# Loading and splitting the second-stage forget-gate weights at another place in a one-core hybrid decoder layer

## The chip, the cores and the metric

The kernel runs on one core of one Trainium2 chip. The metric is device time in microseconds (us) of one execution; several executions give a median. Five engines run side by side, each with its own instruction stream in a fixed order: TensorE (PE, with its weight loads shown apart as PEld), VectorE (DVE), ScalarE (ACT), GpSimd (POOL) and SyncE (SP), which here issues most of the DMAs. POOL issues DMAs too, on a queue of its own.

## What is computed

One decoder layer on 256 tokens of width 2048. A combined projection `h @ w_in` feeds two token mixers, a gated linear attention (GLA) and a differential attention; their outputs are gated, merged and projected again. The change touches the forget gate of the GLA, which is computed in two stages: a projection to rank 16, then a small matrix `w2` (16 x 1024).

```python
h = rmsnorm(x, pre_norm_g[l])
proj = h @ w_in[l]
(a_q, a_k, a_v, a_g, a_lr, b_q, b_k, b_v, b_g, m_a, m_b) = jnp.split(proj, offsets, axis=-1)
gk = jax.nn.log_sigmoid((a_lr @ gla_gk_w2[l] + gla_gk_b[l]).astype(jnp.float32)) / GATE_LOGIT_NORMALIZER
o_a = gla_chunked(
...
merged = jax.nn.sigmoid(m_a) * y_a + jax.nn.sigmoid(m_b) * y_b
out = merged @ w_out[l]
x = x + rmsnorm(out, post_norm_g[l])
```

## The kernel before

Every weight comes from DRAM as float32 and is split on the core into two parts for TensorE: `hi`, a rounded copy that ACT makes (line 263), and `lo = raw - hi`, which DVE makes (line 264). Inputs are split in the same way (`xs`), and a product is three matmuls: hi by hi, hi by lo, lo by hi. The unit of this work is a half tile: one `hi` and one `lo` of 128 x 832 elements in the first phases. `emit_half` makes one; `take` keeps three ahead of the matmuls (`AHEAD = 3`); there are three buffers for each of `raw`, `hi` and `lo`. A `raw` buffer holds two half tiles and is loaded again, on SP's queue, when DVE has made both `lo` parts.

The phases that matter here are the first ones:

- `first_joint` (line 428): 16 half tiles of `v0`, which holds the rank-16 columns and the first values. PE runs 12 matmuls for each (line 440).
- `token_major` (line 466, matmuls on line 452) for `v2` and then `v3`, 8 half tiles each. Between two half tiles `pump` advances side tasks that stand in the list `tasks`.
- From there the phase of the sets: `block_products`, whose weights go through four `chain` buffers (`a` and `b`, loaded by `link`, line 177), interleaved with `others`.

The side tasks are `load_constants` (line 323: identity, biases, masks, and at its end `w2`), `late` (norms and lambda), `forget_gate` (line 521) and `sum_operands` (line 597), which makes sums of blocks of the inputs (`temp`, in `chain` buffers) and splits them into `s4`, `r1`, `s2` and `r3` (lines 617 and 618).

`forget_gate` turns the rank-16 result (`lr`, line 526), splits it into `lrt` (lines 529 to 533), splits `w2_raw` into `w2_s` and `w2h` (lines 537 to 539: two ACT instructions and one DVE instruction that needs the second of them), multiplies (line 548, 8 matmuls of 256 columns), and evaluates the log-sigmoid on ACT and DVE (lines 551 to 564). `w2_raw` is 128 x 1024: the 16 rows of `w2` stand in it four times, at partitions 0, 32, 64 and 96, for the four combinations of hi and lo, and the other rows are zero.

A scheduling layer places each instruction in its engine's order when the program is built, by its dependencies and by what each engine has before it; `tc.keep_in_program_order` pins an instruction to the place that the code gives it. Tiles of one `tag` share a buffer: `w2_raw` has that of `s2h`, `w2h` that of `r3h`. DMAs that SP issues pass through eight completion counters in turn (DMAHW0 to 7), and an issue first waits until the DMA eight places before it has landed. In the profile's rows digits are left out of names: `w_raw` is `w2_raw`, `w_s` is `w2_s`, `w2h` stays.

Of the kernel before, what the change touches and what calls it, by code (L numbers as in the profile page):

```python
# [6 lines left out]
F32 = mybir.dt.float32  # L7
# [3 lines left out]
AF = mybir.ActivationFunctionType  # L11
ALU = mybir.AluOpType
AX = mybir.AxisListType

P = 128
# [7 lines left out]
RANK = 16  # L23
# [71 lines left out]
def hybrid_kernel(ctx: ExitStack, tc, xt, xn, preg, postg, w, w2, gkb, glag, lamv, diffg, ident_d, causal_d, lmask_d, out):  # L95
    nc = tc.nc
    pe, act, dve, pool, sp = nc.tensor, nc.scalar, nc.vector, nc.gpsimd, nc.sync
# [8 lines left out]
    blocks = joint.enter_context(tc.tile_pool(name="blocks", bufs=2))  # L106
# [3 lines left out]
    def u(shape, name, dtype=F32):  # L110
        count[0] += 1
        return big.tile(shape, dtype, tag="u", name=f"{name}_{count[0]}")

    def u2(shape, name, dtype=F32):
        count[0] += 1
        return pools[1].tile(shape, dtype, tag="u2", name=f"{name}_{count[0]}")

    def sm(shape, name, dtype=F32, bufs=2):
        count[0] += 1
        return pools[0].tile(shape, dtype, tag=name, name=f"{name}_{count[0]}", bufs=bufs)  # L120

    def t2(shape, name):
        count[0] += 1
        return pools[0].tile(shape, F32, tag="t2", name=f"{name}_{count[0]}", bufs=5 if len(pools) == 1 else 12)
# [12 lines left out]
    def ps(tag):  # L137
        count[0] += 1
        return psum.tile([P, 512], F32, tag=tag, name=f"{tag}_{count[0]}")

    def f32(ap):
        return ap.bitcast(F32)
# [175 lines left out]
    diffg_s = const.tile([P, 1], F32, name="diffg_s")  # L318
    lam_s = sm([P, 4, 64], "lam_s", bufs=1)

    w2_tile = []

    def load_constants():
        tc.keep_in_program_order(sp.dma_start(ident, ident_d))
        for t, src in ((gkb_s, gkb), (glag_s, glag), (diffg_s, diffg), (causal, causal_d)):
            tc.keep_in_program_order(sp.dma_start(t, src))
        tc.keep_in_program_order(sp.dma_start(lam_s, lamv.partition_broadcast(P)))
        yield
        for n in range(0, len(LEVELS) + 2, 4):
            m = min(4, len(LEVELS) + 2 - n)  # L330
            t = u([P, 4, S], "lmask")
            tc.keep_in_program_order(sp.dma_start(t[:, :m, :], lmask_d[:, n : n + m, :]))
            pool.tensor_copy(lmask[:, n : n + m, :], t[:, :m, :])
            yield
        w2_tile.append(lend("s2h", "w2_raw"))
        tc.keep_in_program_order(dve.memset(w2_tile[0], 0.0))
        for i in range(4):
            pool.dma_start(w2_tile[0][32 * i : 32 * i + RANK, :], w2)

    ones = const.tile([P, P], F32, name="ones")  # L340
    dve.memset(ones, 1.0)
# [36 lines left out]
    def norm_row():  # L378
        bank = ps("bg")
        for b in range(2):  # L380
            diag = sm([P, P], "diag")
            dve.tensor_scalar(out=diag, in0=ident, scalar1=rstd[:, b : b + 1], scalar2=None, op0=ALU.mult)
            pe.matmul(bank[:, P * b : P * b + P], ones, diag, start=True, stop=True)
        dve.tensor_copy(rstd_bc, bank[:, :S])

    def lam():
        late = tc.keep_in_program_order
        prod = sm([P, 2, 64], "lamp", bufs=1)
        for i in range(2):
            late(dve.tensor_tensor(out=prod[:, i, :], in0=lam_s[:, 2 * i, :], in1=lam_s[:, 2 * i + 1, :], op=ALU.mult))  # L390
        dots = sm([P, 2], "lamd", bufs=1)
        dve.tensor_reduce(out=dots, in_=prod, op=ALU.add, axis=AX.X)
        late(act.activation(dots, dots, AF.Exp))
        dve.tensor_scalar(out=neg_lam, in0=dots[:, 1:2], scalar1=dots[:, 0:1], scalar2=-LAM_INIT, op0=ALU.subtract, op1=ALU.add)
        dve.tensor_scalar(out=diffg_s, in0=diffg_s, scalar1=1.0 - LAM_INIT, scalar2=None, op0=ALU.mult)
# [120 lines left out]
    def lend(tag, name, dtype=F32):  # L516

        count[0] += 1
        return blocks.tile([P, 8, P], dtype, tag=tag, name=f"{name}_{count[0]}", bufs=1).rearrange("p a t -> p (a t)")

    def forget_gate():
        w2_raw = w2_tile[0]
        yield
        bank = ps("bg")
        for b in range(2):
            pe.transpose(bank[:, P * b : P * b + P], lr[:, b, :], ident)
        top = t2([P, 512], "lrh").bitcast(F32R)
        lrt = sm([P, S], "lrt", F32R, bufs=1)
        act.activation(top[:, :S], bank[:, :S], AF.Copy)
        for i in (0, 64):  # L530
            act.activation(lrt[i : i + 32, :], bank[i : i + 32, :S], AF.Copy)
            r = slice(i + 32, i + 64)
            dve.tensor_tensor(out=lrt[r, :], in0=bank[r, :S], in1=f32(top[r, :S]), op=ALU.subtract)
        w2_s = lend("s2l", "w2_s", F32R)
        top = lend("r3h", "w2h", F32R)
        r = slice(64, P)
        act.activation(w2_s[:64, :], w2_raw[:64, :], AF.Copy)
        act.activation(top[r, :], w2_raw[r, :], AF.Copy)
        dve.tensor_tensor(out=w2_s[r, :], in0=w2_raw[r, :], in1=f32(top[r, :]), op=ALU.subtract)
        yield  # L540
        gp.extend(u([P, 2, 4, P], "gp") for _ in range(2))
        for hf in range(2):
            for c in range(2):
                bank = ps("bg")
                for i in range(2):
                    ct = 4 * hf + 2 * c + i
                    o = bank[:, S * i : S * i + S]
                    pe.matmul(o, w2_s[:, P * ct : P * ct + P], lrt, start=True, stop=True)
                for i in range(2):
                    ct = 4 * hf + 2 * c + i  # L550
                    act.activation(gp[hf][:, :, 2 * c + i, :], bank[:, S * i : S * i + S].rearrange("p (b t) -> p b t", b=2), AF.Identity, bias=gkb_s[:, ct : ct + 1])
            yield
        e = [lend(tag, "e") for tag in ("r3h", "r3l")]
        z = [t.rearrange("p b c t -> p (b c t)") for t in gp]
        for hf in range(2):
            act.activation(e[hf], z[hf], AF.Abs)
            yield
            act.activation(e[hf], e[hf], AF.Exp, scale=-1.0)
            yield
        for hf in range(2):  # L560
            act.activation(e[hf], e[hf], AF.Ln, bias=1.0)
        for hf in range(2):
            yield
            dve.scalar_tensor_tensor(out=z[hf], in0=z[hf], scalar=0.0, in1=e[hf], op0=ALU.min, op1=ALU.subtract)
        done.add("gate")
# [71 lines left out]
    def late():  # L637
        norm_row()
        yield
        lam()  # L640
        yield

    tasks.append(load_constants())
    first_groups(first_joint())
    tasks.append(late())
    tasks.append(forget_gate())
    tasks.append(sum_operands())
    start = 2 * VG[0] - RANK
# [285 lines left out]
    for g in range(4):  # L934
        banks = token_major(f"ag{g}", 512, x_ops, 2)
        t = u2([P, 2, 512], "ua")
# [187 lines left out]
    for g in range(4):  # L1124
        banks = token_major(f"y1{g}", 512, b_ops, 1 if g else 2, None if g else settle)
        for b in range(2):
            t = gb[g][:, b, :]
# [11 lines left out]
    for b in range(2):  # L1139
        xres.append([])  # L1140
        for i in range(2):
            t = u([P, 1024], "xres")
# [126 lines left out]
```

## Time and profile before

| | |
|---|---|
| median of 3 runs | 1119.35 us (1118.45 to 1119.95) |
| span of the profiled execution | 1121.6 us |
| PE busy | 1101.9 us, 98% of the span |
| DVE busy | 851.3 us, 76% |
| ACT busy | 673.9 us, 60% |
| POOL busy | 111.2 us, 10% |
| DMA | 266.16 MB, mean 237 GB/s |
| PE's waits for other engines, all listed | 4.2 + 2.9 + 1.6 + 1.4 + 1.0 + 0.2 us |

The profiled execution is one of its own: its span, 1121.6 us, stands 2.25 us above the median of the runs. Durations come from the profile, differences are taken within it, and they are then laid on the median. A row of the timeline gives the start in us, the time from the first start to the last end, engine, line of the source, operation, tiles (out<-in), shape and count; in brackets is the idle time of the engine before it and what ended that. A row of the windows gives a stretch and, for each engine, its busy time in it; PEclk is the share of full clock that TensorE was granted there.

### The profile page before, as it was taken

Reading aid. Unit: us, or ns where it says so; the run is one execution under the profiler, and the core shown is the slowest. Engines: PE = TensorE matmul, PEld = TensorE weight load, DVE = VectorE, ACT = ScalarE, POOL = GpSimd, SP = SyncE. Lnnn points to the kernel's source line nnn. Section 1 sums busy time; section 2 is a strip of 40 time slices with the busy share of each in tenths; the row PEclk is TensorE's granted clock in tenths of the full one; section 3 lists DMA queues with packets and bytes.
Section 4 is the critical chain, followed back from the end, with each engine's and each line's share of the span. In section 5 each row is a group of like instructions: output and inputs, shape, how many; then the busy total and the mean of one; then the engine's idle time right before and its main releaser. Section 6 shows DMA issues by size and latency. Waiting matters only on the chain. (4 is left out here: it accounts for less than half of the span.)

```text
span 1121.6 us, 15155 instructions
## 1 busy us (share of the span) xinstructions
PE 1101.9 (98%) x5546; PEld 944.8 (84%) x5546; DVE 851.3 (76%) x1185; ACT 673.9 (60%) x975; POOL 111.2 (10%) x172
## 2 busy tenths in 40 slices
PE   8989999999999999999999999999999999999997
PEld 7989888888888888888888888888888788888886
DVE  6786987978979889799898757958676764665463
ACT  7886666666666656666555555757575643444460
POOL 0201111121021210210200000010101010000000
PEclk9999999999999999999999999999999999999999
DMA  8979959789798897974945675858568575556752
GB/s 318 301 233 317 289 219 317 178 274 302 262 312 220 302 229 230 320 221 163 337 152 179 210 256 174 271 198 270 196 198 255 196 262 201 187 184 214 271 200 75
DMA packets 54042, 266.16 MB, mean 237 GB/s; under 512 B 6672, under 2 KB 8208, under 8 KB 34512
## 3 DMA queue, kind: packets, MB, share of 16 engines
q1 hardware_dynamic: 34848, 188.11, 48.5%
q0 software_dynamic: 18112, 75.77, 24.3%
q10 hardware_dynamic: 1008, 1.32, 0.4%
q8 instruction: 43, 0.70, 0.2%
q14 instruction: 31, 0.25, 0.1%
HBM read 244.20 MB, written 20.97 MB: 236 GB/s over the span
## 5 line engine op out<-in xcount | busy, mean ns | idle before, releaser
L263 ACT ACTIVATE hi<-raw 128x1024 fp32r<-128x1024 f32 (+3 forms) x291 | 299.5, 1033 | 316.8 <-PE mm L452 212.3
L264 DVE TENSOR_TENSOR lo<-raw,hi 128x1024 fp32r<-128x1024 f32 (+3 forms) x291 | 345.3, 1189 | 179.4 <-ACT hi L263 175.8
L452 PE MATMUL mm<-hi,xs 128*128 128x512 f32 (+1 forms) x864 | 218.7, 388 | 0.2 <-ACT hi L263 0.2
L452 PEld LDWEIGHTS mm<-hi,xs 128*128 128x128 f32 x864 | 160.6, 189 | 26.9 <-ACT hi L263 0.5
L452 PE MATMUL bg<-xs,hi 128*128 128x512 f32 x512 | 131.9, 389 | 0.0
L264 DVE TENSOR_TENSOR lo<-a,hi 128x1024 fp32r<-128x1024 f32 x96 | 115.8, 1219 | 10.2 <-ACT hi L263 8.9
L452 PE MATMUL mm<-lo,xs 128*128 128x512 f32 (+1 forms) x432 | 119.6, 384 | 0.1
L263 ACT ACTIVATE hi<-a 128x1024 fp32r<-128x1024 f32 x96 | 101.7, 1060 | 26.2 <-PE mm L452 23.4
L452 PEld LDWEIGHTS bg<-xs,hi 128*128 128x128 f32 x512 | 96.3, 188 | 18.7
L452 PEld LDWEIGHTS mm<-lo,xs 128*128 128x128 f32 x432 | 81.4, 189 | 15.2 <-DVE lo L264 0.4
L452 PEld LDWEIGHTS bg<-xs,lo 128*128 128x128 f32 x512 | 69.8, 190 | 5.0
L452 PE MATMUL bg<-xs,lo 128*128 128x256 f32 x512 | 71.4, 282 | 0.0
L452 PE MATMUL mm<-xs,hi 128*128 128x512 f32 x256 | 67.3, 394 | 0.0
L264 DVE TENSOR_TENSOR lo<-b,hi 128x1024 fp32r<-128x1024 f32 x48 | 57.8, 1222 | 7.8 <-ACT hi L263 7.0
L263 ACT ACTIVATE hi<-b 128x1024 fp32r<-128x1024 f32 x48 | 50.8, 1060 | 15.4 <-PE mm L452 13.6
L452 PEld LDWEIGHTS mm<-xs,hi 128*128 128x128 f32 x256 | 46.1, 189 | 7.6
L452 PE MATMUL mm<-hi,oah 128*128 128x512 f32 x128 | 50.9, 398 | 0.0
L452 PE MATMUL mm<-hi,obh 128*128 128x512 f32 x128 | 50.4, 394 | 0.0
L452 PE MATMUL mm<-hi,oal 128*128 128x512 f32 x128 | 50.3, 393 | 0.0
L452 PE MATMUL mm<-hi,obl 128*128 128x512 f32 x128 | 49.9, 390 | 0.0
L996 ACT ACTIVATE prob<-prob,mx,score_scale 128x128 f32<-128x128 f32 x64 | 34.1, 536 | 10.9 <-DVE mx L991 10.9
L452 PE MATMUL mm<-hi,mh 128*128 128x512 f32 x96 | 37.5, 390 | 0.0
(286 smaller groups left out, 1874.6 us busy)
## 6 DMA issues: line engine op xcount, KB each, us to landing
raw<-in_w_dram SPq DMA_DIRECT2D x128, 1024.0 KB, 5.2
c<-in_w_dram SPq DMA_DIRECT2D x24, 512.0 KB, 10.2
a<-in_w_dram POOLq DMA_DIRECT2D x24, 512.0 KB, 12.1
b<-in_w_dram POOLq DMA_DIRECT2D x24, 512.0 KB, 8.4
raw<-in_w_dram SPq DMA_DIRECT2D x14, 832.0 KB, 6.9
a<-in_w_dram POOLq DMA_DIRECT2D x10, 1024.0 KB, 5.2
b<-in_w_dram POOLq DMA_DIRECT2D x10, 1024.0 KB, 7.5
kh<-dq SPq DMA_DIRECT2D x16, 256.0 KB, 8.1
```

What stands on the lines that cost most here:

```text
L263: act.activation(hi_t[:, a:b], r[:, a:b], AF.Copy)
L264: dve.tensor_tensor(out=lo_t[:, a:b], in0=r[:, a:b], in1=f32(hi_t[:, a:b]), op=ALU.subtract)
L452: i = pe.matmul(*args, **kw)
L996: act.activation(prob[m][:, lo:up], prob[m][:, lo:up], AF.Exp, scale=score_scale[:, b : b + 1], bias=mx[:, i : i + 1], accum_out=z[:, i : ...
```

## The change

The clearing of `w2_raw` moves from DVE, at the end of `load_constants`, to POOL at the start of the program, and the tile is taken from its pool there instead of being borrowed late. The four loads of `w2` move from POOL's queue, at the end of `load_constants`, to SP's queue, as the first four DMAs of that task. The three instructions that split `w2_raw` are pinned to program order.

```diff
-    w2_tile = []
+    w2_tile = [blocks.tile([P, 8, P], F32, tag="s2h", name="w2_raw", bufs=1).rearrange("p a t -> p (a t)")]
+    pool.memset(w2_tile[0], 0.0)
 
     def load_constants():
+        for i in range(4):
+            tc.keep_in_program_order(sp.dma_start(w2_tile[0][32 * i : 32 * i + RANK, :], w2))
         tc.keep_in_program_order(sp.dma_start(ident, ident_d))
...
-        w2_tile.append(lend("s2h", "w2_raw"))
-        tc.keep_in_program_order(dve.memset(w2_tile[0], 0.0))
-        for i in range(4):
-            pool.dma_start(w2_tile[0][32 * i : 32 * i + RANK, :], w2)
...
         r = slice(64, P)
-        act.activation(w2_s[:64, :], w2_raw[:64, :], AF.Copy)
-        act.activation(top[r, :], w2_raw[r, :], AF.Copy)
-        dve.tensor_tensor(out=w2_s[r, :], in0=w2_raw[r, :], in1=f32(top[r, :]), op=ALU.subtract)
+        late = tc.keep_in_program_order
+        late(act.activation(w2_s[:64, :], w2_raw[:64, :], AF.Copy))
+        late(act.activation(top[r, :], w2_raw[r, :], AF.Copy))
+        late(dve.tensor_tensor(out=w2_s[r, :], in0=w2_raw[r, :], in1=f32(top[r, :]), op=ALU.subtract))
```

Up to the end of the first phases the order of instructions moves on several engines. On ACT, in `v2`, around the split of `w2_raw` (lines 537 and 538; 617 are splits of sums, 551 the gate's first evaluation), before:

```order
L531 ACTIVATE lrt_604<-bg_600 32x256
L537 ACTIVATE w_s_610<-w_raw_514 64x1024
L263 ACTIVATE hi_681<-raw_615 128x832
L617 ACTIVATE r1h<-temp_765 128x1024
L538 ACTIVATE w2h_611<-w_raw_514 64x1024
L263 ACTIVATE hi_704<-raw_679 128x832
L263 ACTIVATE hi_727<-raw_679 128x832
L617 ACTIVATE s2h<-temp_765 128x1024
L551 ACTIVATE gp_633<-bg_635,gkb_s 128x2x128 x2
```

and now:

```order
L530 ACTIVATE lrt_604<-bg_600 32x256
L537 ACTIVATE w_s_610<-w_raw 64x1024
L538 ACTIVATE w2h_611<-w_raw 64x1024
L263 ACTIVATE hi_681<-raw_615 128x832
L551 ACTIVATE gp_633<-bg_635,gkb_s 128x2x128 x2
```

The two splits of `w2_raw` follow each other, `hi_681` comes behind them, and the splits `r1h` and `s2h` have gone to places behind the gate, between the `hi` parts `hi_813`, `hi_836` and `hi_857`. On DVE the third split, line 539, stands directly ahead of `lo_682`; before, it stood three instructions behind it.

On PE, the place of the gate's matmuls (line 548) in `v2`, before:

```order
L452 MATMUL mm_548<-hi_645,xs_81 128x416 x2
L452 MATMUL mm_549<-hi_645,xs_81 128x416 x2
L452 MATMUL mm_548<-lo_646,xs_81 128x416
L452 MATMUL mm_549<-lo_646,xs_81 128x416
L452 MATMUL mm_548<-lo_646,xs_81 128x416
L548 MATMUL bg_635<-lrt_604,w_s_610 128x256 x2
L548 MATMUL bg_640<-lrt_604,w_s_610 128x256 x2
```

and now:

```order
L451 MATMUL mm_549<-hi_617,xs_80 128x416 x2
L451 MATMUL mm_548<-lo_618,xs_80 128x416
L451 MATMUL mm_549<-lo_618,xs_80 128x416
L548 MATMUL bg_635<-lrt_604,w_s_610 128x256 x2
L548 MATMUL bg_640<-lrt_604,w_s_610 128x256 x2
```

They stand one half tile earlier: behind the second `lo` matmul of half tile `hi_617`, where before they stood behind the third `lo` matmul of the next one, 13 matmuls of 416 columns later.

On SP's queue, the constants between two loads of weights, before:

```order
L226 DMA raw_374<-in_w_dram 128x1664
L324 DMA ident<-in_ident_dram 128x128
L326 DMA gkb_s<-in_gkb_dram 128x8
L326 DMA glag_s<-in_glag_dram 128x4
L326 DMA diffg_s<-in_diffg_dram 128x1
L326 DMA causal<-in_causal_dram 128x384
L327 DMA lam_s_99<-in_lamv_dram 128x256
L226 DMA raw_421<-in_w_dram 128x1664
```

and now:

```order
L226 DMA raw_376<-in_w_dram 128x1664
L326 DMA w_raw<-in_w_dram 16x1024 x4
L327 DMA ident<-in_ident_dram 128x128
L329 DMA gkb_s<-in_gkb_dram 128x8
L329 DMA glag_s<-in_glag_dram 128x4
L329 DMA diffg_s<-in_diffg_dram 128x1
L329 DMA causal<-in_causal_dram 128x384
L330 DMA lam_s_99<-in_lamv_dram 128x256
L226 DMA raw_427<-in_w_dram 128x1664
```

Four issues stand ahead of the constants, so ten instead of six lie between the two loads of weights, and the DMA eight places before `raw_427` is now the third load of `w2`. Later on the same queue, the first `b` load of the sets stands behind the two `raw` loads of 128 x 1600 instead of ahead of them, since its buffer is that of the `temp` which `s2` is split from; the next `raw` loads and the loads `c` behind them keep their number, with one `raw` now ahead of three `c`. Behind that the orders are the same.

## The prediction

> **What bounds the kernel now.** I read the page's totals first, then the list of PE's waits, the timeline around the longest of them that the change touches, and the windows for the clock there.
>
> ```profile
> span 1121.6 us, 15155 instructions
> ...
> PE 1101.9 (98%) x5546; PEld 944.8 (84%) x5546; DVE 851.3 (76%) x1185; ACT 673.9 (60%) x975; POOL 111.2 (10%) x172
> ...
> PE bg L985 <- ACT kh L968: 4.2, 4, 2.5
> PE bg L548 <- DVE w_s L539: 2.9, 1, 2.9
> ```
>
> PE is busy for 98% of the span: TensorE is the bound, and other work costs time only where PE stands still or runs slowly. There is little of that, and one piece belongs to the tile that is changed: line 548, the gate's matmuls, waits 2.9 us once for line 539, the last split of `w2_raw`. PE's timeline around it:
>
> ```profile
> 57.62 1.68 PE L452 MATMUL mm<-hi,xs 128*128 128x416 f32 x8
> 59.14 0.92 PE L452 MATMUL mm<-lo,xs 128*128 128x416 f32 x4
> 59.90 1.67 PE L452 MATMUL mm<-hi,xs 128*128 128x416 f32 x8
> 61.41 0.72 PE L452 MATMUL mm<-lo,xs 128*128 128x416 f32 x3
> 64.99 1.15 PE L548 MATMUL bg<-lrt,w_s 128*128 128x256 f32 x8 [2.86 <-DVE w_s L539]
> 66.17 2.96 PE L452 MATMUL mm<-hi,xs 128*128 128x416 f32 x8
> 69.99 1.68 PE L452 MATMUL mm<-hi,xs 128*128 128x416 f32 x8
> ```
>
> The start times matter here, since matmuls overlap. A half tile of 8 + 4 matmuls takes 59.90 - 57.62 = 2.28 us, 0.19 us a matmul. The half tile behind the wait takes 69.99 - 66.17 = 3.82 us for the same 12. The windows say why:
>
> ```profile
> core 0: us, PE busy (x) PEld busy (x) DVE busy (x) ACT busy (x) POOL busy (x), PEclk, DMA share, GB/s
> 66.10:69.60 3.50, 3.50 (x12) 3.35 (x11) 3.50 (x5) 3.50 (x9) 0.00 (x0) 0.51 0.34 78
> 69.60:72.00 2.40, 2.40 (x14) 2.37 (x13) 1.96 (x3) 2.40 (x4) 0.00 (x0) 1.00 0.96 300
> 768.00:774.00 6.00, 5.39 (x36) 4.68 (x36) 6.00 (x24) 3.72 (x10) 0.00 (x0) 1.00 1.01 308
> 880.00:884.00 4.00, 4.00 (x16) 3.36 (x16) 3.25 (x18) 2.95 (x8) 0.00 (x0) 0.76 0.38 156
> ```
>
> PE's granted clock was 0.51 in the 3.5 us behind the gate's matmuls and 1.00 again afterwards. So the wait has a second price, paid after it. The two other windows follow waits for `kh`: the longest (2.5 us, ending at 877) was followed by a clock of 0.76 in the window from 880, one of the short ones (near 769) by no drop. What makes the wait is seen on ACT, DVE and POOL:
>
> ```profile
> 51.26 1.93 POOL L338 DMA_DIRECT2D w_raw<-in_w_dram  x4 [2.46 <-DVE w_raw L336]
> 55.82 0.38 ACT L531 ACTIVATE lrt<-bg 32x256 fp32r<-32x256 f32 x1
> 59.48 1.06 ACT L537 ACTIVATE w_s<-w_raw 64x1024 fp32r<-64x1024 f32 x1 [3.28 <-DMA w_raw<-in_w_dram]
> 60.45 0.88 ACT L263 ACTIVATE hi<-raw 128x832 fp32r<-128x832 f32 x1
> 61.23 1.04 ACT L617 ACTIVATE r1h<-temp 128x1024 fp32r<-128x1024 f32 x1
> 62.30 1.05 ACT L538 ACTIVATE w2h<-w_raw 64x1024 fp32r<-64x1024 f32 x1
> 64.97 1.05 ACT L617 ACTIVATE s2h<-temp 128x1024 fp32r<-128x1024 f32 x1
> 63.62 1.22 DVE L539 TENSOR_TENSOR w_s<-w_raw,w2h 64x1024 fp32r<-64x1024 f32 x1
> ```
>
> POOL issues the `w2` loads only at 51.3, ACT stands 3.28 us until they land, and two foreign instructions (`hi`, `r1h`) stand between the splits 537 and 538, so line 539 ends at 64.84.
>
> **What the change removes.** (a) The wait. Without it the first gate matmul would have started one step after the third `lo`: 61.41 + 3 x 0.19 = 61.98; it started at 64.99. That is 3.0 us. (b) The slow clock behind it: 3.82 - 2.28 = 1.54 us. Together 4.55 us, if line 548 finds its operand ready.
>
> [...]
>
> **What it leaves.** (c) Line 548 stands 13 matmuls earlier now, behind the second `lo` at 59.14, so PE is there at 59.14 + 2 x 0.19 = 59.52. Is line 539 done? ACT ends `lrt` at 56.20 and finds `w2_raw` loaded over 20 us ago; 537 takes 60.45 - 59.48 = 0.97 us to the next start, 538 starts at 57.17 and ends 1.05 us later, 58.22. DVE, which before was busy until it took line 539, starts it some 0.05 us later and ends at 58.25 + 1.22 = 59.5. From its end to the first matmul the trace has 64.99 - 64.84 = 0.15 us: 59.65. PE waits 0.1 us. Bounds: 0, and 1.1 us if DVE has one `lo` more ahead; a wait of that size is like that at 769, without a drop of the clock. I take 0.1.
>
> (d) ACT next. It is the engine that comes late afterwards already now:
>
> ```profile
> 78.38 2.54 ACT L263 ACTIVATE hi<-raw 128x832 fp32r<-128x832 f32 x3
> 79.40 1.78 PE L452 MATMUL mm<-hi,xs 128*128 128x416 f32 x8 [0.19 <-ACT hi L263]
> 81.25 1.02 PE L452 MATMUL mm<-lo,xs 128*128 128x416 f32 x4
> ```
>
> PE starts that half tile (the first of `raw_787`) 0.3 us late, and its `lo` part about 0.2 us late (79.40 + 8 x 0.19 = 80.9, 0.1 of the difference being the slow first step). With PE 4.4 us ahead, it wants this `hi` at 79.1 - 4.4 = 74.7. From 537 to this `hi` ACT needed 78.38 - 59.48 = 18.9 us, nearly without a gap. Now it starts at 56.20, `r1h` and `s2h` (2.1 us) are put behind, but it has to stand about 1.2 us for the first gate matmuls (from 58.9, the end of `hi_681`, to 60.1: an estimate, the first two of eight matmuls that take 1.15 us in all): 56.20 + 18.9 - 2.1 + 1.2 = 74.2, plus 0.9 for the instruction itself, 75.1. PE waits 0.4 us there; DVE, behind line 564 and the split of `s4`, is late by as much again. Together 0.8 against 0.5 now: 0.3 us are given back. Bounds: -0.5 (all these small waits gone) and +1.5 (one ACT instruction of 1 us and half of another in the way).
>
> **What it moves at no cost.** Clearing on POOL at the start lies in that engine's idle time:
>
> ```profile
> 39.25 0.70 POOL L360 TENSOR_TENSOR rstd<-ssq,neg_half 128x2 f32<-128x2 f32 x1 [38.16 <-DVE ssq L369]
> ```
>
> POOL stands 38.16 us before this row. DVE is rid of a memset at 50 us that only the loads waited for. The loads on SP's queue are the item to look at:
>
> ```profile
> 26.51 0.42 SPq L324 DMA_DIRECT2D ident<-in_ident_dram  x1
> 29.00 0.43 SPq L327 DMA_DIRECT2D lam_s<-in_lamv_dram  x1
> 30.33 0.33 SPq L226 DMA_DIRECT2D raw<-in_w_dram  x1
> 32.94 0.80 SPq L332 DMA_DIRECT2D lmask<-in_lmask_dram  x2
> raw<-in_w_dram SPq DMA_DIRECT2D x1, 832.0 KB, 7.6
> 41.01 0.88 ACT L263 ACTIVATE hi<-raw 128x832 fp32r<-128x832 f32 x1
> 45.64 1.67 PE L452 MATMUL mm<-hi,xs 128*128 128x416 f32 x8
> ```
>
> Four issues at the constants' pace (six from 26.51 to 29.43, 0.49 us each) are 2 us. But an issue also waits for the landing of the DMA eight places before. `diffg` now waits for `raw_374`, which the first `lmask` waited for until 32.94; then `causal`, `lam` and the next `raw` follow at 33.4, 33.9 and 34.4, waiting for loads of `w2` that have landed with it. The next `raw` goes out at about 34.5 instead of 30.33, 4.2 us late. It takes 7.6 us at most (the row of that one issue), less with an emptier queue: it lands at 42 at the latest instead of 37.9. ACT reads it at 41.01, PE not before 45.64, so the cover is 7.7 us less 1.2 for the two splits' lead: 6.5 us against 4.2. Without cover each further us would be a us of PE. Taken at 0. The `lmask` and the next `raw` fall back by 1 to 2 us on the queue and find their own cover of the same kind.
>
> The first `b` load moves from 70.38 to behind the split of `s2`, about 80:
>
> ```profile
> 70.38 0.33 SPq L177 DMA_DIRECT2D b<-in_w_dram  x1
> 85.17 0.33 SPq L226 DMA_DIRECT2D raw<-in_w_dram  x1
> 98.55 1.06 ACT L263 ACTIVATE hi<-b 128x1024 fp32r<-128x1024 f32 x1 [0.51 <-PE mm L452]
> 102.63 0.87 ACT L263 ACTIVATE hi<-raw 128x800 fp32r<-128x800 f32 x1 [1.12 <-PE bg L452]
> raw<-in_w_dram SPq DMA_DIRECT2D x1, 800.0 KB, 10.7
> ```
>
> It is wanted by ACT at 98.55 - 4.1 = 94.4, and 80 plus 10.7 us, the time of the `raw` that stands in the same crowd, is 90.7. That `raw` itself is issued at about 83, lands with 1 MB more ahead at the latest at 83 + 10.7 + 4 = 97.7, and is read at 98.5. Covered, though barely. Taken at 0.
>
> **Sum.** -3.0 - 1.55 + 0.1 + 0.3 = -4.15. The profiled execution would come to 1121.6 - 4.15 = 1117.45, and the median to 1119.35 - 4.15 = **1115.2 us**, since behind this place PE is the bound and the order is the same. Own range: 1114.0 (small waits gone too, 5.35) to 1116.4.
>
> **Rivals.**
>
> 1. The slow clock is not there in the runs of the median, or comes back behind the new small waits. Then only the wait is won: 3.0 - 0.4 = 2.6, 1116.75 us. For it: the drop is one observation in one execution. Against: two waits of 2.5 and 2.9 us, two drops.
> 2. ACT takes over as the bound in `v3`: the side tasks pile up behind the gate, and PE stands at the half tiles of `raw_787` and `raw_834` for 2 us more than I worked out. 4.15 - 2 = 2.15, 1117.2 us; with more, 1118. For it: ACT has hardly a gap from 59.48 to 81. Against: it starts 3.3 us earlier and has two splits fewer before the critical `hi`.
> 3. The change doesn't do what it says: line 539 comes late for another reason (the `lrt` split, an ACT instruction that waits), and the wait stays at some 2.5 us with its drop. About 1119 us.
> 4. Slower: the load queue becomes the bound from 84 to 105, with the `b` load in the crowd. From the point where that `raw` lands later than 98.5 + 2.5 (ACT's lead of a half tile), each us is lost, and a stop over 2.5 us costs 1.5 more. To lose all, PE must stand 4.15 - 1.5 + 2.5 = 5.2 us there: landing at 106, 23 us after its issue, twice the row's 10.7. Price 1122. For it: 1 MB more in the fullest stretch. Against: three `c` loads have stepped behind a `raw` there.
>
> **How the numbers follow.** Forecast 0.60, rivals 0.14, 0.14, 0.05, 0.07. A change under 0.2%, 2.2 us, can't be told from none here: faster means below 1117.1, slower above 1121.6. Faster: 0.60 + 0.11 of rival 1 + 0.04 of rival 2 = 0.75. Same: 0.03 + 0.10 + 0.05 = 0.18. Slower: 0.07. The range takes in rivals 1 and 2: 1113.8 to 1118.2.
>
> **What would show it.** Line 548 starts near 59.6 with a wait under 0.5 us in the list of PE's waits; the granted clock stays at 1.00 from 55 to 75; the `raw` load goes out near 34.5 and PE shows no wait at 45.6; the half tile of `raw_787` starts near 75 with 0.3 to 0.6 us of wait for ACT. I am wrong if PE waits over 1 us between 70 and 105, if a wait for `raw` or `b` stands in ACT's rows there and reaches PE, or if the stretch is 4 us shorter and the end is not.

## The result, and the profile after

| | before | changed |
|---|---|---|
| median of the runs (20 each, one chip) | 1119.43 us | 1116.89 us |
| lowest to highest | 1116.53 to 1123.67 | 1114.86 to 1119.30 |
| ratio | | 0.9977, interval 0.9969 to 0.9986 |
| profiled execution: span | 1121.6 us | 1114.1 us |

The changed kernel is 2.5 us faster (0.9977 x 1119.43 = 1116.9; the interval is 1.6 to 3.5 us). The forecast was 4.15 us and 1115.2 us, with a range of 1113.8 to 1118.2. Two more comparisons, on chips 9 and 3 further down, gave 0.9981 and 0.9974. The two profiled spans differ by much more, 7.5 us, and part of that has nothing to do with the change, as will be seen.

First the list of PE's waits, changed kernel (in total, how many, the longest):

```profile
PE bg L985 <- ACT kh L968: 4.7, 4, 3.0
PE bg L345 <- DVE ones_b L342: 1.6, 1, 1.6
PE bg L986 <- DVE kl L969: 0.8, 3, 0.3
PE bg L439 <- ACT hi L263: 0.6, 1, 0.6
PE mm L451 <- ACT hi L263: 0.3, 1, 0.3
```

The entry for line 548, 2.9 us, is gone. PE's timeline around that line, and then around the half tile of `raw_787` (its row is the one that waits for ACT), both of the changed kernel:

```profile
55.90 1.68 PE L451 MATMUL mm<-hi,xs 128*128 128x416 f32 x8
57.42 0.54 PE L451 MATMUL mm<-lo,xs 128*128 128x416 f32 x2
58.05 1.18 PE L548 MATMUL bg<-lrt,w_s 128*128 128x256 f32 x8
59.07 0.55 PE L451 MATMUL mm<-lo,xs 128*128 128x416 f32 x2
59.45 1.68 PE L451 MATMUL mm<-hi,xs 128*128 128x416 f32 x8
61.71 1.68 PE L451 MATMUL mm<-hi,xs 128*128 128x416 f32 x8
```

```profile
73.55 1.78 PE L451 MATMUL mm<-hi,xs 128*128 128x416 f32 x8 [0.34 <-ACT hi L263]
```

Line 548 starts 0.25 us after PE could have (57.42 + 2 x 0.19 = 57.80; DVE ends line 539 at 57.90), and a half tile behind it takes 61.71 - 59.45 = 2.26 us, full pace. The windows confirm the clock:

```profile
55.00:62.00 7.00, 6.91 (x40) 6.53 (x39) 6.87 (x10) 5.92 (x12) 0.00 (x0) 1.00 0.71 281
62.00:66.10 4.10, 4.10 (x24) 4.06 (x23) 3.17 (x4) 4.10 (x6) 0.00 (x0) 1.00 0.13 52
66.10:69.60 3.50, 3.50 (x20) 3.46 (x19) 2.22 (x5) 3.50 (x7) 0.88 (x2) 1.00 0.69 237
```

SP's queue at the start, changed kernel:

```profile
24.49 0.33 SPq L226 DMA_DIRECT2D raw<-in_w_dram  x1
24.91 1.78 SPq L326 DMA_DIRECT2D w_raw<-in_w_dram  x4
31.11 0.33 SPq L329 DMA_DIRECT2D diffg_s<-in_diffg_dram  x1
32.50 0.38 SPq L226 DMA_DIRECT2D raw<-in_w_dram  x1
```

The four loads take 1.78 us to issue, `diffg` stands until 31.11, and the next `raw` goes out at 32.50. Everything in this execution from PE's first half tile of `v2` on lies 1.74 us earlier for a reason at the very start (43.90 against 45.64), so that is 34.24 on the clock of the earlier profile, where 34.5 was forecast. PE does not wait for that load.

Where did the time go? The starts of the same half tiles, read off PE's timelines:

| PE starts | before | changed | earlier by | won in the stretch |
|---|---|---|---|---|
| first half tile of `v2` | 45.64 | 43.90 | 1.74 | 1.74 |
| half tile of `raw_787` | 79.40 | 73.55 | 5.85 | 4.11 |
| line 985, third wait for `kh` | 821.89 | 816.07 | 5.82 | 0.0 |
| line 985, longest wait for `kh` | 877.37 | 871.70 | 5.67 | -0.15 |
| end of the span | 1121.6 | 1114.1 | 7.5 | 1.8 |

The stretch of the change wins 4.11 us; the sum forecast 4.15. The 1.74 and the 1.8 us are for the most part two slow stretches of the clock, one behind PE's wait for `hi` that ends at 7.6 us, the other behind the longest wait for `kh`. Before had both (granted clock 0.52 from 8.2 to 11.7 us and from 878.6 to 882.1 us), the changed execution neither (1.00 from 6 to 1109 us), though its wait for `kh` was the longer one (3.0 against 2.5 us). That is luck of the execution; the experiment with a pause by itself has such cases side by side. The open question was why the median shows 2.5 us and the stage 4.1, and whether the slow clock behind line 548 is the difference.

### The profile page after: what moved, and what is told of

Read it like the earlier page. It is cut to its first block, busy times and chain, and to the rows that moved or that the text cites. A ratio compares the mean times of both kernels' runs of the same rounds, so it can differ in the third digit from the quotient of the medians.

```text
span 1114.1 us, 15149 instructions
## 1 busy us (share of the span) xinstructions
PE 1097.9 (99%) x5546; PEld 941.2 (84%) x5546; DVE 849.7 (76%) x1184; ACT 673.6 (60%) x975; POOL 110.7 (10%) x169
## 5 line engine op out<-in xcount | busy, mean ns | idle before, releaser
L263 ACT ACTIVATE hi<-b 128x1024 fp32r<-128x1024 f32 x48 | 50.8, 1060 | 15.3 <-PE mm L451 13.6
```

The lines of the kernel that those rows point to most:

```text
L263: act.activation(hi_t[:, a:b], r[:, a:b], AF.Copy)
```

## The experiments

Four theories were put against each other. P is the prediction: the slow clock behind the wait is a loss of 1.5 us of its own (theory 1 below is P for every execution). Theory 2: that slow clock comes in some executions only, so that only the wait is sure to be won. Theory 3: the late `raw` on SP's queue costs time. Theory A came up with the first of the experiments.

**The pins alone.** Before, with the pins of the change:

```diff
-        act.activation(w2_s[:64, :], w2_raw[:64, :], AF.Copy)
+        late = tc.keep_in_program_order
+        late(act.activation(w2_s[:64, :], w2_raw[:64, :], AF.Copy))
...
```

> Before, with the three splits kept in program order and nothing else changed; every engine's order stays that of before. It serves as a second look at before. Both theories: same time as before within 1 us, and the wait of 2.9 us at the gate's matmuls is there again. Theory 1 (the slow clock behind that wait belongs to it in every execution): the granted clock is near 0.5 for some 3.5 us behind the wait again. Theory 2 (the slow clock comes in part of the executions, so that only the wait is won for certain): about an even chance that the clock stays at 1.00 behind it, and the span is then 1.5 us shorter there. The same look at the start and at the longest wait for kh gives two more draws.

Measured: ratio 0.9998 (0.9986 to 1.0011); the pins alone do nothing. Its profile was the surprise. PE's timeline, around line 548 (here 549) and around `raw_787`:

```profile
62.81 1.18 PE L549 MATMUL bg<-lrt,w_s 128*128 128x256 f32 x8 [2.36 <-DVE w_s L540]
63.83 0.35 PE L452 MATMUL mm<-lo,xs 128*128 128x416 f32 x1
64.02 1.68 PE L452 MATMUL mm<-hi,xs 128*128 128x416 f32 x8
66.28 1.68 PE L452 MATMUL mm<-hi,xs 128*128 128x416 f32 x8
```

```profile
74.61 0.91 PE L452 MATMUL mm<-lo,xs 128*128 128x416 f32 x4
77.23 1.76 PE L452 MATMUL mm<-hi,xs 128*128 128x416 f32 x8 [1.71 <-ACT hi L263]
```

The wait is there and no slow clock follows it (66.28 - 64.02 = 2.26 us). But PE then stands 1.71 us for the `hi` of `raw_787`, where it stood 0.19 in the first profile. From the first gate matmul to that half tile it is 77.23 - 62.81 = 14.42 us; with the slow clock it was 79.40 - 64.99 = 14.41. ACT's timeline of the same execution says why:

```profile
63.86 3.04 ACT L552 ACTIVATE gp<-bg,gkb_s 128x256 f32<-128x256 f32 x8
66.73 2.06 ACT L557 ACTIVATE e<-gp 128x1024 f32<-128x1024 f32 x2
68.62 1.11 ACT L559 ACTIVATE e<-e 128x1024 f32<-128x1024 f32 x1
69.57 0.95 ACT L263 ACTIVATE hi<-raw 128x832 fp32r<-128x832 f32 x1
70.36 1.11 ACT L559 ACTIVATE e<-e 128x1024 f32<-128x1024 f32 x1
71.31 0.81 ACT L580 ACTIVATE vh<-mm,rstd 128x208 fp32r<-128x208 f32 x2
71.94 0.97 ACT L263 ACTIVATE hi<-raw 128x832 fp32r<-128x832 f32 x1
72.73 0.82 ACT L580 ACTIVATE vh<-mm,rstd 128x208 fp32r<-128x208 f32 x2
73.36 2.08 ACT L562 ACTIVATE e<-e 128x1024 f32<-128x1024 f32 x2
75.26 1.13 ACT L618 ACTIVATE s4h<-temp 128x1024 fp32r<-128x1024 f32 x1
76.20 2.55 ACT L263 ACTIVATE hi<-raw 128x832 fp32r<-128x832 f32 x3
```

From the gate's first evaluation (line 551, here 552), at 63.86, ACT has no gap until that `hi` at 76.20. The length of ACT's chain sets the start of the half tile, and PE's slow steps lie beside it. That is theory A.

**The loads alone.** The changed kernel without the pins (those lines as in before). The scheduling layer then puts the splits earlier, and line 548 (here 547) into an earlier half tile.

> The changed kernel without the three pins: the weights are loaded in the first microseconds, the splits stand where the planner puts them, about 10 us earlier, and the gate's matmuls go into an earlier half tile. If the gain comes from the loads alone, it is as fast as the changed kernel, 1116 to 1118 us, 2 to 3 us under before, with no wait at the gate's matmuls. If the pins carry it, because the early splits push a split of the weights that is due sooner, PE waits for ACT at a half tile between 45 and 60 us, and half of the gain or more is lost: 1118 to 1119.5 us.

Measured: 1117.94 us beside 1120.34 for before, ratio 0.9968 (0.9955 to 0.9981). The ratio on record is not the quotient of the two medians, which is 0.9979 here; both lie in the interval. PE waits 0.15 us at the gate, for `lrt`:

```profile
55.30 1.18 PE L547 MATMUL bg<-lrt,w_s 128*128 128x256 f32 x8 [0.15 <-DVE lrt L532]
```

The early loads carry the gain; the pins are not needed for it.

**The loads on POOL's queue.**

```diff
-            tc.keep_in_program_order(sp.dma_start(w2_tile[0][32 * i : 32 * i + RANK, :], w2))
+            tc.keep_in_program_order(pool.dma_start(w2_tile[0][32 * i : 32 * i + RANK, :], w2))
```

> The changed kernel with the four loads of w2 on POOL's queue instead of SP's, so that SP issues the constants and the next raw as before (near 29 instead of 32.5 us). My theory, that the 4 us by which SP's raw came late are hidden and that the missing 1.6 us of the forecast are the slow clock: same as the changed kernel within 0.8 us. Rival (theory 3): the raw that comes late costs something in the runs that were not profiled; then it is 1.0 to 1.6 us faster than the changed kernel, about 1115.3 us.

Measured: 1117.18 us, ratio 0.9968 (0.9955 to 0.9981), on the same chip and with the same runs of before as the last one. SP's `raw` goes out at 30.46 instead of 32.50. With `v2` starting at 45.57 here and at 43.90 there, that is 3.7 us earlier on one clock:

```profile
30.46 0.43 SPq L226 DMA_DIRECT2D raw<-in_w_dram  x1
```

The changed kernel itself was not run on that chip. Against the kernel without pins, whose SP queue has the same order as that of the change, no gain can be told (1117.18 against 1117.94 us, and the same ratio), and no profile of the change shows PE waiting for that load. Theory 3 has nothing for it. By time alone the run is not a clean test, because the scheduling layer also put line 548 seven matmuls further forward than in the change.

**A pause by itself.** The core of a kernel of its own: groups of matmuls, and between two of them one DVE and one ACT instruction that PE must wait for, with eight lengths of ACT's instruction in turn.

```python
m = work.tile([P, 4096], F32R, tag="m", name=f"m_{g}")
late(act.activation(m[:, :n], flat[:, :n], AF.Copy, scale=gate))
...
pe.matmul(bank[:, :416], hold[:, c : c + P], m[:, :416], start=i == 0, stop=i == busy - 1)
...
late(dve.tensor_scalar(out=gate, in0=bank[:, :1], scalar1=0.0, scalar2=1.0, op0=ALU.mult, op1=ALU.add))
```

> Not this layer at all: it leaves the whole computation out and copies its input to the output. 64 groups of 44 to 56 matmuls of 128x416 (9 to 11 us), and between two groups PE waits for one DVE and one ACT instruction, so that it stands for about 1 to 5 us, eight lengths in turn. Counted is behind which pauses the matmuls step at half pace. Theory 1 (a pause of 2.5 us or more always brings the slow clock, a shorter one never): a sharp edge between 2 and 2.5 us, all of the pauses of about 3 us followed by steps near 0.38 us. Theory 2 (a matter of where the pause falls): of the pauses of 2 to 3.4 us some are followed by slow steps and some not, with the share rising with the length; at 2.9 us between a quarter and three quarters of them.

Counted over PE's 63 pauses, by the steps between the starts of the matmuls behind each (0.19 us at full pace, 0.35 slow):

| pause, us | 1.08 | 1.50 | 1.93 | 2.36 | 2.7 to 2.8 | 3.2 | 3.6 | 4.1 |
|---|---|---|---|---|---|---|---|---|
| pauses | 8 | 7 | 8 | 8 | 8 | 8 | 8 | 8 |
| followed by slow steps | 0 | 0 | 4 | 3 | 6 | 7 | 8 | 8 |

Two pauses of the same length in PE's timeline, taken from two stretches of it:

```profile
202.82 12.05 PE L129 MATMUL bank<-m,hold 128*128 128x416 f32 x56 [2.78 <-ACT m L124]
```

```profile
753.50 6.82 PE L129 MATMUL bank<-m,hold 128*128 128x416 f32 x34 [2.78 <-ACT m L124]
```

The same pause, and slow steps behind the first alone. So theory 1's sharp edge in the length of the pause falls: of the pauses from 1.9 to 3.2 us some are followed by the slow clock and some not. PE's windows behind these two pauses, and one of another slow stretch:

```profile
202.80:206.30 3.50, 3.48 (x11) 3.37 (x12) 0.00 (x0) 0.00 (x0) 0.00 (x0) 0.58 0.00 0
753.50:757.00 3.50, 3.50 (x18) 3.41 (x19) 0.00 (x0) 0.00 (x0) 0.00 (x0) 1.00 0.02 5
271.30:276.90 5.60, 5.54 (x16) 5.29 (x17) 0.00 (x0) 0.01 (x1) 0.00 (x0) 0.50 0.00 0
```

The granted clock was 0.58 in the 3.5 us behind the first pause and 1.00 behind the second. In the third window it was 0.50, and PE took 16 matmuls in 5.6 us, 0.35 us each; at 0.16 us more than at full pace that is 2.6 us. So the length of a pause of 1.9 to 3.2 us does not tell whether the slow clock follows, which is theory 2 as far as the clock goes.

**Before again, twice.** Unchanged.

> Before once more, unchanged. In the profile of before the half tile of raw_787 starts 14.41 us after the first gate matmul with the slow clock in between, in that of the pinned one 14.42 us without it. Theory A (ACT, which stands behind the gate's evacuation without a gap until the hi of raw_787, sets that start, and the slow clock lies beside it): 14.4 us again within 0.2, whichever clock comes; without the slow clock PE waits 1.5 to 2 us for that hi, with it 0.2 to 0.5. Theory P (the prediction: the slow clock is a loss of its own of 1.5 us): 14.4 us with it, 12.9 without.

> Before, unchanged, for the same question. B: 2.0 to 2.6 us at the longest wait for kh; chance: 1.9 to 3.2. The stage takes 44.2 to 44.8 us from the first half tile of v2 to the second of set0, and the half tile of raw_787 starts 14.4 us after the first gate matmul (theory A).

The first gave 0.9998 (0.9984 to 1.0012), the second 1.0004 (0.9991 to 1.0017), as they should. Rows of PE's timeline and a window with the clock behind the wait (0.57 and 0.56), first of the one, then of the other:

```profile
65.10 1.55 PE L548 MATMUL bg<-lrt,w_s 128*128 128x256 f32 x8 [2.96 <-DVE w_s L539]
```

```profile
79.51 0.83 PE L452 MATMUL mm<-hi,xs 128*128 128x416 f32 x3 [0.17 <-ACT hi L263]
```

```profile
66.00:69.60 3.60, 3.60 (x15) 3.48 (x14) 3.11 (x5) 3.58 (x10) 0.00 (x0) 0.57 0.22 54
```

```profile
62.38 1.66 PE L548 MATMUL bg<-lrt,w_s 128*128 128x256 f32 x8 [2.24 <-DVE w_s L539]
```

```profile
76.78 1.78 PE L452 MATMUL mm<-hi,xs 128*128 128x416 f32 x8 [0.16 <-ACT hi L263]
```

```profile
62.40:66.00 3.60, 3.60 (x15) 3.50 (x16) 3.00 (x4) 3.57 (x10) 0.00 (x0) 0.56 0.27 113
```

79.51 - 65.10 = 14.41 and 76.78 - 62.38 = 14.40 us, this time both with a slow clock behind the wait. With 14.41 and 14.42 that makes four profiles, in which 14.4 us holds whichever clock came: A, not P. The stage of the second, 44.02 us, lies just under the expected 44.2 to 44.8.

**One ACT instruction less, in before.**

```diff
-            act.activation(hi, t, AF.Copy)
+            if name == "s4":
+                pool.tensor_copy(hi, t)
+            else:
+                act.activation(hi, t, AF.Copy)
```

> Before with the hi of s4 made on POOL instead of ACT, one ACT instruction of about 1 us less between the gate and the hi of raw_787; PE's order stays. Theory A: without the slow clock the half tile of raw_787 starts 13.4 us after the first gate matmul instead of 14.4, and 1 us is won; with the slow clock PE is the later one, 14.1 to 14.3 us, and 0.1 to 0.3 are won. Theory P: it changes nothing, 14.4 with and 12.9 without.

```profile
63.23 1.18 PE L548 MATMUL bg<-lrt,w_s 128*128 128x256 f32 x8 [2.58 <-DVE w_s L539]
64.44 2.85 PE L452 MATMUL mm<-hi,xs 128*128 128x416 f32 x8
```

```profile
77.33 1.68 PE L452 MATMUL mm<-hi,xs 128*128 128x416 f32 x8
```

These rows of PE's timeline show the slow clock (8 matmuls in 2.85 us) and no wait for ACT at `raw_787`: 77.33 - 63.23 = 14.10 us. With ACT's chain shorter, PE with its slow steps is the later of the two, at the price A had named. The time of the runs, 0.9991 (0.9979 to 1.0002), can't show 0.3 us. The case without the slow clock, 13.4 us, did not come up.

**The changed kernel again, and with one ACT instruction less.** The second with the same edit to `s4`.

> The changed kernel once more, unchanged. Theory A: the stage from the first half tile of v2 to that of raw_787 takes 34.6 us again (38.2 to 38.7 in before), so 3.6 to 4.1 us are won in each execution, and the median comes out 3 to 3.6 us under before. Theory 2 (the slow clock behind the gate's wait is what varies, and only the wait is won for certain): 2.2 to 2.8 us under before. Runs with a mean clock of 0.998 (no slow stretch) stand 3.3 us apart in the runs so far; A has them at 3.6, theory 2 at 2.6.

> The changed kernel with the hi of s4 on POOL, as above. In the changed kernel the half tile of raw_787 starts 15.50 us after the first gate matmul, and PE waits 0.34 us there for ACT. Theory A: 15.0 to 15.1 us, no wait for ACT there, and 0.4 to 0.5 us less in the stage (34.2 us), which the time of the runs can hardly show. [...]

The changed kernel: 0.9981 (0.9971 to 0.9992), 2.1 us under before by that ratio and 2.6 by the medians (1118.42 against 1121.05). The 34.6 us of the expectation run to the first half tile of `raw_834`, two half tiles behind `raw_787`; they came out at 34.64. With `s4` on POOL: 0.9965 (0.9951 to 0.9978), and its PE timeline has

```profile
59.78 0.95 PE L548 MATMUL bg<-lrt,w_s 128*128 128x256 f32 x6
```

```profile
74.03 0.92 PE L451 MATMUL mm<-lo,xs 128*128 128x416 f32 x4
74.78 1.67 PE L451 MATMUL mm<-hi,xs 128*128 128x416 f32 x8
```

15.00 us instead of 15.50, and the wait for ACT is gone. So ACT still set this start by a hair in the changed kernel. The stage won as A had it in the profiles, but the median, which A put 3 to 3.6 us under before, came out 2.1 to 2.6 us under it: a miss.

**Is the rest lost at `kh`?** In three profiles of the changed order PE stood 2.9 to 3.2 us at the longest wait for `kh`, in the profiles of before 2.0 to 2.7. Theory B made that the missing piece.

> The changed kernel, unchanged, for the part of the gain that is missing: the stage up to the second half tile of set0 wins 3.6 to 4.2 us in every profile, the runs show 2.5. Theory B: the rest is lost at the longest wait for kh, near the end. There the load of one raw lands 0.0 to 0.3 us behind the mark in three profiles of the changed order and 0.2 to 0.9 us ahead of it in the four of before, so that PE stands 2.9 to 3.2 us instead of 2.0 to 2.7, and more often pays the slow clock behind it. B: again 2.9 to 3.2 us here. Chance (the landing varies from execution to execution and the three were unlucky): anywhere from 1.9 to 3.2. Median 2 to 3 us under before in either case.

> The changed kernel once more, one look, as a further draw for theory B: 2.9 to 3.2 us at the longest wait for kh; chance: 1.9 to 3.2, with at least one of this and the run before below 2.7.

Rows of PE's timeline, first of the one, then of the other:

```profile
871.19 0.44 PE L985 MATMUL bg<-kh,q 128*128 128x128 f32 x2 [2.19 <-ACT kh L968]
```

```profile
872.38 0.44 PE L985 MATMUL bg<-kh,q 128*128 128x128 f32 x2 [3.03 <-ACT kh L968]
```

2.19 us in one, 3.03 in the other, and 2.6 in the third profile of before: B as stated, always 2.9 to 3.2 us, fell. The wait changes from execution to execution in either kernel. What sets it is on record: in all 13 profiles of the layer the wait is the landing of one `raw` load, counted from one matmul ahead of it, plus 2.82 to 2.85 us. That load was 12.5 us on its way where the wait was 1.9 us, and 13.6 to 14.3 us where it was 3.0 to 3.2. Why it varies was not tried. The first of the two gave the third comparison, 1117.27 us beside 1120.06, ratio 0.9974 (0.9964 to 0.9985).

**Both side steps together.** `w2` on POOL's queue and the `hi` of `s4` on POOL.

> A version meant to be better than both: the loads of w2 on POOL's queue and the hi of s4 on POOL as well. Stage from the first half tile of v2 to the second of set0 38.9 to 39.2 us (40.55 in the changed kernel, 39.58 with s4 alone, 39.25 with the loads alone), no wait of PE for ACT at the half tiles of raw_787 and raw_834; the median 1.0 to 1.6 us under the changed kernel on the same chip.

Measured: 1117.11 us, ratio 0.9973 (0.9961 to 0.9985), beside 1117.27 for the changed kernel on the same chip. The expectation had 1.0 to 1.6 us between the two: a miss. The stage took 39.24 us, no less than with the loads on POOL's queue alone (39.25). PE's start at `raw_787` had no wait for ACT left that the second step could remove, as the row of that kernel shows:

```profile
74.36 1.68 PE L451 MATMUL mm<-hi,xs 128*128 128x416 f32 x8
```

That is 1.3 us less in the stage than the changed kernel, and 0.2 us in the median. It may be a second case in which a gain in this stage does not come out whole, but the two intervals are over 1 us wide to either side, and the runs can't tell 0.2 from 1.3 us. No version was shown to be better than the change; `s4` on POOL alone has the best ratio, but its interval overlaps.

## Why the prediction was right, and where it was not

The starts in all the profiles, in us from PE's first half tile of `v2`:

| kernel | its start | to line 548 | line 548 to `raw_787` | to the second half tile of set 0 |
|---|---|---|---|---|
| before | 45.64 | 19.35 | 14.41 | 44.66 |
| before, again | 45.64 | 19.46 | 14.41 | 44.77 |
| before, third | 43.65 | 18.73 | 14.40 | 44.02 |
| pins alone, no slow clock | 43.96 | 18.86 | 14.42 | 44.16 |
| before, `s4` on POOL | 44.16 | 19.07 | 14.10 | 43.62 |
| changed | 43.90 | 14.15 | 15.50 | 40.55 |
| changed, again | 45.76 | 14.15 | 15.50 | 40.56 |
| changed, third | 44.16 | 14.13 | 15.48 | 40.53 |
| changed, fourth | 43.91 | 14.12 | 15.50 | 40.51 |
| changed, `s4` on POOL | 45.65 | 14.12 | 15.00 | 39.58 |
| no pins | 43.91 | 11.39 | 17.82 | 39.66 |
| `w2` on POOL's queue | 45.57 | 12.55 | 16.24 | 39.25 |
| `w2` and `s4` on POOL | 45.12 | 12.55 | 16.24 | 39.24 |

- **(a), the wait: right.** It is gone in all profiles of the change. It was worth 2.2 to 3.0 us, by the execution.
- **(c), 0.1 us left at line 548:** 0.25 us, within its bounds.
- **(d), ACT late at `raw_787`, 0.3 us given back: right.** PE waits 0.34 us there. The start was forecast near 75 and came at 73.55, which is 75.29 with the 1.74 us of the start phase added.
- **SP's queue at no cost: right as far as shown.** The `raw` came out 0.3 us from where it was put, and PE has no wait behind it. For the `b` load no wait of PE showed up either.
- **(b), 1.54 us for the slow clock: the step that failed.** "So the wait has a second price, paid after it" took PE's slow steps for a loss. In before ACT reaches the `hi` of `raw_787` 14.4 us after line 548 in any case, so without the slow clock PE stands 1.71 us instead of 0.19. The sum still met the profile, since the change takes away that wait too: without a slow clock the waits of 2.36 and 1.71 us, 4.1 together, become 0.25 and 0.34, which gives 3.5, and the stage shows 44.16 - 40.54 = 3.6 us. The 4.1 us of the first two profiles have 0.5 more from the longer way to line 548 (19.35 against 18.86), not from the slow clock; the third profile of before has a slow clock and gives 44.02 - 40.54 = 3.5. The right way to write the term was "PE at line 548 comes 5.2 us earlier (19.35 - 14.15), and ACT's way from there to `raw_787` becomes 1.1 us longer (15.50 - 14.41)".
- **Rival 1** had the time of the median (1116.75 against 1116.89) by a mechanism that the runs do not bear out. An execution without the slow clock wins 3.6 us in the stage, not 2.6. Rivals 2 to 4 are out by the list of waits: nothing at line 548, 0.3 us at `raw_787`, and no wait of PE between 76 and 105 us.
- **The range: in part luck.** The median lies 1.7 us above the forecast and outside the prediction's own range, 1114.0 to 1116.4. It lies in 1113.8 to 1118.2 because that takes in rivals 1 and 2, neither of which the profiles show. Of the signs of being wrong the last one came true in part: the stretch is 4 us shorter, and the end, by the medians, only 2.5.
- **Two sums do not come out.** With the small waits gone, bound -0.5 in place of +0.3 and 0 in place of 0.1 give 5.05 us, not 5.35. In rival 4 a stop of 4.15 - 1.5 = 2.65 us loses all, with the landing near 103.7; the 5.2 us and 106 belong to its price of 1122. Neither changes the forecast.
- **"the median to 1119.35 - 4.15": this did not hold.** The stage wins 3.5 to 4.3 us between any two profiles, 3.9 on average (44.40 - 40.54), and the three comparisons of runs give 2.5, 2.1 and 2.9, each with an interval of about 1 us to either side. Some 1.4 us are missing, and the cause stays open. Part of the spread is seen: the start of `v2` varies from 43.65 to 45.64 us in before and from 43.90 to 45.76 in the change, and the longest wait for `kh` from 2.0 to 2.6 and from 2.2 to 3.0, with or without a slow clock behind each. The wait for `kh` is 0.4 us longer on average in the change (2.76 against 2.36). But four profiles of each can't show a difference of 1 us in these places. The changed profile, with no slow stretch before its last 5 us, has a mean clock of 0.998; of the runs of the last comparison with 0.998 or more, before has 1118.7 us (7 runs) and the change 1115.8 (5 runs), 2.9 us apart, still less than 3.6.

A trace of the covered slow clock can be seen in the same runs. The first profile of before, with three slow stretches (windows from 8.2, 66.1 and 878.6 us at 0.51 or 0.52), has a mean clock of 0.994, the changed one with none 0.998; one stretch would give 0.996 or 0.997, an estimate from these two. At 0.996 or 0.997 instead of 0.998 or more, before is slower by 0.6, 1.0 and 0.8 us on average on three chips, the changed kernel by 1.7 (first comparison) and 2.1 us (third). That fits a before in which the slow stretch often lies behind line 548, beside ACT, and a change in which only the uncovered ones are left.

## What to carry to other kernels

Before a slow or idle stretch of the bounding engine is counted as a gain, follow the next engine from the same point to the next place where the two meet. If the time between the two points is the same with and without the stretch, it is covered, and the gain ends where the other engine's chain ends. A gain read from one pair of profiles should be taken from a stretch between two marks, and be put against several executions before it is moved to the median, where other places varied here by up to 2 us (the start of `v2`), against a gain of 2.5. And whether a pause was followed by a slow clock in one profile says little about the next execution: here the slow clock followed 20 of 32 pauses of 1.9 to 3.2 us.

## What was not expected of the hardware

- In the run with a pause by itself the slow clock followed 4 of 8 pauses of 1.93 us and 6 of 8 of about 2.8 us, none of 15 pauses up to 1.50 us, and each of 16 of 3.6 us or more. One profile can't tell whether a pause of 2 to 3 us has a price in the next execution.
- The same stage, with the same order, came out within 0.05 us in four profiles (40.51 to 40.56), while the whole span varied from 1113.6 to 1117.8 us: the spread lies in a few places, not in the work.
- Near the longest wait for `kh` one `raw` load was issued 13.4 to 14.0 us ahead of the same matmul in every profile, and landed between 0.93 us ahead of it and 0.32 us behind it: 1.25 us of spread in one transfer, with the same orders on all queues from the sets on.
